# 399 pairs of unread matmuls behind the last sum of squares of an encoder, with weights at sixteen places

## The chip, the cores and the metric

The kernel runs on one core of one Trainium2 chip. The metric is the time of one execution on the device in microseconds. Four compute engines matter: TensorE (PE in the profile; its weight loads are shown as PEld), VectorE (DVE), ScalarE (ACT) and the queue that issues DMAs (SP). GpSimd (POOL) does almost nothing.

## The reference, cut to what matters

The reference is a trunk of two encoder layers on 256 tokens of width 2048, in float32. The end is what the change touches:

```
for i in range(DEPTH):                                   # DEPTH = 2
    h = rmsnorm(x, g_mix[i]);  z = h @ w_in[i]           # then two attentions, gates, w_out
    gu = rmsnorm(x, g_ffn[i]) @ w_gate_up[i]
    x = x + (silu(gate) * up) @ w_down[i]                # D_FF = 5632
    e = p[i] @ w_ple_in[i]
    x = x + sigmoid(rmsnorm(x, g_ple[i]) @ w_ple_gate[i]) * e
return rmsnorm(x, g_final)                               # x * rsqrt(mean(x * x) + eps) * g
```

## The kernel before

The state x is kept transposed in `xT`: 16 chunks of 128 rows (features) by 256 columns (tokens). Each operand of a matmul is a float32 value split into two parts, a rounded high part and the rest: `ua[j]` and `ub[j]` hold one chunk each, 256 columns of high part and then 256 of low part.

A product of weights and activations is written by `product`. It takes the weights in pieces of at most eight blocks of 128x128. For each piece, `piece` issues a DMA into `w` (tag `w32`, four buffers), ACT copies it rounded into `whi` (three buffers, L176), and DVE writes the rest to `wlo` (three buffers). `emit` then issues two matmuls per block, the pair that this document speaks of:

```
PE.matmul(acc, hi[:, s], u, start=start, stop=False)                 # L206: 512 columns
PE.matmul(acc[:, T:], lo[:, s], u[:, :T], start=False, stop=stop)    # L207: 256 columns
```

The first operand after the bank is the stationary one, the weights; `s` starts at a multiple of 128 elements. The bank `acc` is one of four in the pool `ps_mm`. `joined` adds its two halves with the help of ACT. The very last product of the kernel is written with three matmuls of 256 columns per block instead (L202 to L204), so that no joining is needed behind it. In `values` the roles are exchanged: there the activations (`ua`) are the stationary operand and the weights stream (L387 to L389).

The order of the instructions on each engine is made by a scheduler that simulates the program while it is built; a buffer that is asked for again waits until its last reader is done. Each engine works through its own list in order.

The kernel ends like this. In the second layer's last loop each chunk of `xT` gets its last addition, ACT squares it (L258, for the last chunk L255), DVE adds the squares, and ACT scales the chunk by the final gain (L678). `norm` sums over the partitions with four matmuls of one column (L266) and takes the inverse root on DVE; `spread` brings it to all partitions with a matmul by `ones` (L275). Then DVE multiplies `xT` by it in six parts, and each part is sent out by a DMA (L699).

Of the kernel before, what the change touches and what calls it, by code (L numbers as in the profile page):

```python
# [13 lines left out]
F32R = mybir.dt.float32r  # L14
I32 = mybir.dt.int32
AF = mybir.ActivationFunctionType
# [3 lines left out]
P = 128  # L20
T = 256
DM = 2048
NC = DM // P
# [13 lines left out]
PT = 8  # L37
# [13 lines left out]
def encoder(ctx, tc, x, p, positions, cols, lams, wq, wk, wv, wcq, wckv, wkr, wga, wgb,  # L51
            w_q_up, w_kn, w_v, w_bd, w_bm, w_out, w_gate, w_up, w_down, w_pin, w_pg, rope_c, out):
    nc = tc.nc
    V, A, PE = nc.vector, nc.scalar, nc.tensor
# [3 lines left out]
    wts = pool("wts")  # L58
    tmp = pool("tmp")
    stat = pool("stat")  # L60
    ps_mm = pool("ps_mm", 4, space=PSUM)
# [6 lines left out]
    def bank(ps=ps_at, tag="at", name="at", shape=(P, 2 * T)):  # L68
        return ps.tile(list(shape), F32, tag=tag, name=name)

    def tt(o, a, b, op):
        return V.tensor_tensor(out=o, in0=a, in1=b, op=op)  # L72
# [4 lines left out]
    def ts(o, a, s1, s2, op0, op1=ALU.bypass):  # L77
        return V.tensor_scalar(out=o, in0=a, scalar1=s1, scalar2=s2, op0=op0, op1=op1)  # L78


    ua = [const.tile([P, 2 * T], F32R, name=f"ua{j}") for j in range(NC)]
# [12 lines left out]
    xT = const.tile([P, NC, T], F32, name="xT")  # L94
# [18 lines left out]
    aside = [fa(j) for j in range(5)]  # L113
    posi = aside[0][:, 0, :].bitcast(I32)
    posf = aside[0][:, 1, :]

    def tables():
        V.tensor_copy(posf, posi)
        got = []
        for i, name in enumerate("pm"):  # L120
            ang, k, r, a = (aside[j + i][:, m, :] for j in (1, 3) for m in range(2))
            ts(ang, posf, rc[:, 2 * i : 2 * i + 1], None, ALU.mult)
            ts(k, ang, 1.0 / TWO_PI, ROUND, ALU.mult, ALU.add)
            ts(k, k, ROUND, None, ALU.subtract)
            stt(r, k, -C1, ang, ALU.mult, ALU.add)
            stt(r, k, -C2, r, ALU.mult, ALU.add)
            stt(r, k, -C3, r, ALU.mult, ALU.add)
            ts(r, r, PI_IN, -PI_IN, ALU.min, ALU.max)
            stt(a, r, -1.0, r, ALU.mult, ALU.min)
            ts(a, a, math.pi / 2, None, ALU.add)  # L130
            cs = const.tile([P, T], F32, name="cos_" + name)
            sn = const.tile([P, T], F32, name="sin_" + name)
            A.activation(cs, a, AF.Sin)
            A.activation(sn, r, AF.Sin)
            ts(sn, sn, rc[:, 2 * i + 1 : 2 * i + 2], None, ALU.mult)
            got += [cs, sn]
        return got
# [71 lines left out]
    def product(src, us, whole=False):  # L209


        acc = bank(ps_mm, "mm", "mm")
        n = len(us)
        for a in range(0, n, PT):
            m = min(PT, n - a)
            hi, lo = piece(src[:, a * P : (a + m) * P], m)
            emit(acc, hi, lo, 0, us[a : a + m], a == 0, a + m == n, whole)
        return acc[:, :T] if whole else acc
# [10 lines left out]
    def joined(acc, o=None):  # L229
        t = scratch("join", 3)  # L230
        A.activation(t, acc[:, T:], AF.Copy)  # L231
        o = scratch("a", 4) if o is None else o
        tt(o, acc[:, :T], t, ALU.add)
        return o
# [7 lines left out]
    def rsqrt(src, n, eps, width):  # L242

        v, y, a = (stat.tile([P, 2 * DH], F32, tag="r" + s, name="r" + s, bufs=2)[:, :width] for s in "vya")
        ts(v, src, 1.0 / n, eps, ALU.mult, ALU.add)
        ts(y.bitcast(I32), v.bitcast(I32), -0.5, 1597463007.0, ALU.mult, ALU.add)
        for _ in range(3):
            stt(a, y, -0.5, y, ALU.mult, ALU.mult)
            tt(a, a, v, ALU.mult)
            stt(y, a, 1.5, y, ALU.add, ALU.mult)  # L250
        return y

    def square_into(acc, src, first):
        if first:
            A.activation(acc, src, AF.Square)  # L255
        else:
            sq = scratch("sq", 2)
            A.activation(sq, src, AF.Square)  # L258
            tt(acc, acc, sq, ALU.add)

    def norm(sums, n):

        s = bank()
        for j, a in enumerate(sums):
            for b in range(2):
                PE.matmul(s[:, b : b + 1], a[:, b * P : (b + 1) * P], ones[:, 0:1], start=j + b == 0, stop=j + b == len(sums))  # L266
        return rsqrt(s[:, 0:2], n, EPS, 2)

    def spread(col, copied=True):

        dg = stat.tile([P, 2, P], F32, tag="dg", name="dg", bufs=1)
        for b in range(2):
            ts(dg[:, b, :], ident, col[:, b : b + 1], None, ALU.mult)
        s = bank()
        PE.matmul(s[:, :T], ones, dg, start=True, stop=True)  # L275
        if not copied:
            return s[:, :T]
        row = stat.tile([P, T], F32, tag="row", name="row", bufs=2)
        A.activation(row, s[:, :T], AF.Copy)  # L279
        return row  # L280

    def normed(sums, one, two):

        got = [joined(one())]
        col = norm(sums, DM)
        got.append(joined(two()))
        return spread(col), col, got
# [4 lines left out]
    def stream(us, gain):  # L292

        acc = squares()

        def add(c):
            split(us[c], xT[:, c, :], g(gain, c))
            square_into(acc, xT[:, c, :], c == 0)

        return acc, add  # L300
# [110 lines left out]
    for L in range(DEPTH):  # L411

        steps = values(wv[L], ua, None if L else load)
        for vd in steps:
            if L == 0 and vd is not None:
# [3 lines left out]
                with after_splits():  # L419
                    rcol = norm([sq0[0][:, j, :] for j in range(2)], DM)  # L420
                    next(steps)
                    R = spread(rcol)
                    cos_p, sin_p, cos_m, sin_m = tables()
                    lambdas()
                break
            if L:
                next(steps)
                rcol = norm([acc], DM)
                next(steps)
                R = spread(rcol)  # L430
                break
# [5 lines left out]
        for o, t in ((cr, cos_p), (sr, sin_p), (crm, cos_m), (srm, sin_m)):  # L437
            tt(o, t, R, ALU.mult)

# [17 lines left out]
        def latent(us, w, raws):  # L457
            ss = squares()
            for c in range(len(us)):
                tt(raws[c], joined(product(w[L, c], ua)), R, ALU.mult)  # L460
                square_into(ss, raws[c], c == 0)
# [55 lines left out]
        def gate(w, store, n):  # L517
            tt(store(n), joined(product(w[L, n], ua)), R, ALU.mult)

# [115 lines left out]
        acc, add = stream(ub, f"g_ffn{L}")  # L635
# [4 lines left out]

        R, _, pre = normed([acc], lambda: product(w_gate[L, 0], ub), lambda: product(w_up[L, 0], ub))
        pT, es = ua[14:], []
# [4 lines left out]
        for part, (f0, f1) in enumerate(FF_PARTS):  # L647
# [11 lines left out]
            if last:  # L659
                acc, add = stream(ub, f"g_ple{L}")  # L660
# [10 lines left out]
        R, _, pre = normed([acc], lambda: product(w_pg[L, 0], ub), lambda: product(w_pg[L, 1], ub))  # L671
# [8 lines left out]
        else:  # L680
            acc, add = stream(ua, f"g_mix{L + 1}")
# [11 lines left out]
            add(n)  # L693

    R = spread(norm(sums, DM), copied=False)
    for n, m in ((0, 1), (1, 1), (2, 2), (4, 4), (8, 4), (12, 4)):
        o = xT[:, n : n + m, :]
        tt(o, o, R[:, None, :].to_broadcast([P, m, T]), ALU.mult)
        nc.sync.dma_start(out[:, n : n + m, :], o)  # L699
# [84 lines left out]
```

## Time and profile before

| | |
|---|---|
| median of 2 runs | 2934.06 us (2933.75 to 2934.36) |
| the profiled execution | 2934.72 us |
| its span, first to last instruction | 2932.9 us |
| PE busy | 2914.7 us, 99% of the span |
| PEld busy | 2550.8 us, 87% |
| DVE busy | 2063.6 us, 70% |
| ACT busy | 1524.5 us, 52% |
| HBM read | 527.43 MB |

The profile is of one execution. A record has a start and a duration; records of matmuls overlap, because a matmul begins before the results of the one ahead have all left the array. So the pace of a stream of matmuls is read from their starts. The granted clock is the share of TensorE's full clock that the chip let it have in a stretch. Some records of matmuls are missing.

### The profile page before, as it was taken

The page shows a single profiled execution, that of the slowest core. Times are in us where ns is not written, and L with a number is a line of the kernel's source. Part 1 is how long each engine was busy: PE and PEld are TensorE (multiplying, and loading weights), DVE is VectorE, ACT ScalarE, POOL GpSimd, SP SyncE. Part 2 cuts the span into 40 slices and gives each one's busy share as a digit, 9 for nine tenths or more (in the row PEclk, how much of TensorE's full clock was granted, in tenths as well). Part 3 has the DMA queues.
Part 4 walks back from the last instruction along what each step waited for, and adds up shares of the span by engine and source line. Part 5 has one row for each costly group of instructions (what it writes and reads, how often), then busy time and mean ns, then how long its engine had stood idle before and what let it go on. Part 6 is the DMA issues. An engine that isn't in the chain of part 4 may idle for free.

```text
span 2932.9 us, 43979 instructions
## 1 busy us (share of the span) xinstructions
PE 2914.7 (99%) x16750; PEld 2550.8 (87%) x16750; DVE 2063.6 (70%) x3529; ACT 1524.5 (52%) x2529; POOL 1.6 (0%) x8
## 2 busy tenths in 40 slices
PE   9999999999999999999999999999999999999998
PEld 7888888888888888888888888888888888888887
DVE  7897658776666666666859975687666666666676
ACT  6676545544444444445646755455444444444454
POOL 0000000000000000000000000000000000000000
PEclk9999999999999999999999999999999999999999
DMA  6444455555565565555554444555555655655654
GB/s 229 166 161 148 158 188 191 187 186 187 183 193 188 178 191 195 187 187 186 187 186 165 150 153 164 189 190 186 187 187 182 192 188 181 194 188 188 188 185 140
DMA packets 156019, 532.40 MB, mean 182 GB/s; under 512 B 16928, under 2 KB 23840, under 8 KB 155808
## 3 DMA queue, kind: packets, MB, share of 16 engines
q1 hardware_dynamic: 155376, 529.01, 54.5%
q8 instruction: 131, 2.15, 0.3%
q14 instruction: 80, 0.66, 0.1%
q10 hardware_dynamic: 432, 0.59, 0.1%
HBM read 527.43 MB, written 2.10 MB: 181 GB/s over the span
## 4 chain that ended last, share of the span: by engine, by line
PE 99%; DVE 1%; DMA 0%; ACT 0%; SPq 0%; issue 0%; DVEq 0%
PE mm L206 61%; PE mm L207 31%; PE S L336 1%; PE mmv L389 1%; PE mmv L387 1%; PE mmv L388 1%; PE at L354 0%; PE at L558 0%; PE at L615 0%; DMA w<-in_wv 0%; PE at L275 0%; DVE xT L72 0%; PE at L266 0%; DVE wlo L72 0%; DVE a L72 0%; PE at L573 0%
## 5 line engine op out<-in xcount | busy, mean ns | idle before, releaser
L72 DVE TENSOR_TENSOR wlo<-w,whi 128x1024 fp32r<-128x1024 f32 (+2 forms) x1029 | 1229.3, 1195 | 761.6 <-ACT whi L176 749.3
L176 ACT ACTIVATE whi<-w 128x1024 fp32r<-128x1024 f32 (+2 forms) x1029 | 1066.0, 1036 | 1336.4 <-issue 783.8
L206 PE MATMUL mm<-ub,whi 128*128 128x512 f32 x3952 | 1391.3, 394 | 0.0
L206 PE MATMUL mm<-ua,whi 128*128 128x512 f32 x3744 | 1320.3, 394 | 0.0
L207 PE MATMUL mm<-ub,wlo 128*128 128x256 f32 x3952 | 1117.7, 283 | 0.0
L207 PE MATMUL mm<-ua,wlo 128*128 128x256 f32 x3744 | 1059.5, 283 | 0.0
L206 PEld LDWEIGHTS mm<-ub,whi 128*128 128x128 f32 x3952 | 742.0, 188 | 170.3
L206 PEld LDWEIGHTS mm<-ua,whi 128*128 128x128 f32 x3744 | 702.5, 188 | 158.1
L207 PEld LDWEIGHTS mm<-ub,wlo 128*128 128x128 f32 x3952 | 743.2, 188 | 0.8
L207 PEld LDWEIGHTS mm<-ua,wlo 128*128 128x128 f32 x3744 | 704.1, 188 | 2.0
L72 DVE TENSOR_TENSOR a<-mm,join 128x256 f32<-128x256 f32 x421 | 175.2, 417 | 0.3 <-ACT join L231 0.2
L231 ACT ACTIVATE join<-mm 128x256 f32<-128x256 f32 x453 | 166.8, 369 | 5.4 <-PE mm L207 5.1
L72 DVE TENSOR_TENSOR xT<-xT,mm 128x256 f32<-128x256 f32 x256 | 106.9, 420 | 49.6 <-PE mm L207 45.8
L72 DVE TENSOR_TENSOR a<-a,row 128x256 f32<-128x256 f32 x207 | 87.3, 424 | 6.6 <-ACT row L279 0.8
L387 PE MATMUL mmv<-whi,ua 128*128 128x512 f32 x128 | 51.5, 403 | 2.6 <-ACT whi L176 2.6
L72 DVE TENSOR_TENSOR a<-a 128x256 f32<-128x256 f32 x120 | 50.9, 425 | 4.0
L388 PE MATMUL mmv<-whi,ua 128*128 128x512 f32 x128 | 50.9, 399 | 0.0
L72 DVE TENSOR_TENSOR ua<-a,ua 128x256 fp32r<-128x256 f32 x120 | 50.1, 417 | 1.0 <-ACT ua L239 1.0
L239 ACT ACTIVATE ua<-a 128x256 fp32r<-128x256 f32 x120 | 48.4, 403 | 2.6 <-DVE a L72 2.6
L389 PE MATMUL mmv<-wlo,ua 128*128 128x512 f32 x128 | 47.7, 405 | 0.1
L345 ACT ACTIVATE E<-S,nm 128x256 f32<-128x256 f32 x96 | 44.2, 470 | 5.1 <-DVE nm L78 5.0
L72 DVE TENSOR_TENSOR ssq<-ssq,sq 128x256 f32<-128x256 f32 x97 | 40.5, 418 | 0.5 <-ACT sq L258 0.5
(153 smaller groups left out, 1160.3 us busy)
## 6 DMA issues: line engine op xcount, KB each, us to landing
w<-in_w_gate SPq DMA_DIRECT2D x176, 512.0 KB, 4.5
w<-in_w_up SPq DMA_DIRECT2D x176, 512.0 KB, 4.5
w<-in_w_down SPq DMA_DIRECT2D x128, 512.0 KB, 3.5
w<-in_wga SPq DMA_DIRECT2D x64, 512.0 KB, 3.7
w<-in_wgb SPq DMA_DIRECT2D x64, 512.0 KB, 4.4
w<-in_w_out SPq DMA_DIRECT2D x64, 512.0 KB, 4.5
w<-in_w_pg SPq DMA_DIRECT2D x64, 512.0 KB, 3.7
w<-in_w_down SPq DMA_DIRECT2D x64, 384.0 KB, 3.5
```

The lines of the kernel that those rows point to most:

```text
L72: return V.tensor_tensor(out=o, in0=a, in1=b, op=op)
L176: last_split[:] = A.activation(hi[:, :m], w[:, :m], AF.Copy), tt(lo[:, :m], w[:, :m], hi[:, :m].bitcast(F32), ALU.subtract)
L206: PE.matmul(acc, hi[:, s], u, start=start, stop=False)
L207: PE.matmul(acc[:, T:], lo[:, s], u[:, :T], start=False, stop=stop)
L231: A.activation(t, acc[:, T:], AF.Copy)
L239: return A.activation(hi, src, AF.Copy), tt(lo, src, hi.bitcast(F32), ALU.subtract)
L336: PE.matmul(S[:, b, :], q[:, b * P : (b + 1) * P], k, start=j == 0, stop=j == len(pairs) - 1)
L345: last_exp[0] = A.activation(E[:, b, :], S[:, b, :], AF.Exp, bias=nm[:, b : b + 1], scale=scale, accum_out=sm[:, b : b + 1])
L387: PE.matmul(banks[b], xh, hi[:, s], start=a + j == 0, stop=False)
L388: PE.matmul(banks[b], xl, hi[:, s], start=False, stop=False)
L389: last_mm[:] = [PE.matmul(banks[b], xh, lo[:, s], start=False, stop=a + j == n - 1)]
```

## The change

A function `others` is called between the last spreading and the six output products. It takes two buffers of the tag of `whi` and two of the tag of `wlo` and lets ACT copy the first four chunks of `xT` (1024 columns) into each of the four. Then it issues 19 groups of 21 pairs of matmuls, 798 in all, in a fixed order. Each group has a bank of its own from the pool of four; nothing reads it.

A pair is as in `emit`: 512 columns of `ua` with a block of weights from the one tile, and 256 columns with a block from the other, into the second half of the bank. The difference is where the block starts. In the kernel it starts at multiples of 128 elements; here it starts `h` elements further for the first matmul of a pair and `l` further for the second. In eleven groups both are the same (96, 104, 112, 120, 0, 8, 16, 32, 48, 64, 80), in five they differ; that makes sixteen places. Three groups more repeat 96, and do 96 and 0 with the second matmul writing the first half of the bank instead of the second. The output of the kernel is not affected.

```
+    def others():
+        N = 21
+        src = xT[:, :4, :].rearrange("p c t -> p (c t)")
+        his = [wts.tile([P, PT * P], F32R, tag="whi", name="side", bufs=3) for _ in range(2)]
+        los = [wts.tile([P, PT * P], F32R, tag="wlo", name="side", bufs=3) for _ in range(2)]
+        for t in his + los:
+            A.activation(t, src, AF.Copy)
+
+        def blocks(name, h, l, low=T):
+            acc = bank(ps_mm, "mm", name)
+            for j in range(N):
+                k = j % 14
+                o = k % 7 * P
+                tc.keep_in_program_order(PE.matmul(acc, his[k // 7][:, o + h : o + h + P], ua[j % NC], start=j == 0, stop=False))
+                tc.keep_in_program_order(PE.matmul(acc[:, low : low + T], los[k // 7][:, o + l : o + l + P], ua[j % NC][:, :T], start=False, stop=j == N - 1))
+
+        for h in (96, 104, 112, 120, 0, 8, 16, 32, 48, 64, 80):
+            blocks(f"both{h}_", h, h)
+        for h, l in ((96, 0), (0, 96), (96, 32), (96, 112), (112, 96)):
+            blocks(f"h{h}l{l}_", h, l)
+        blocks("again96_", 96, 96)
+        blocks("front96_", 96, 96, 0)
+        blocks("front0_", 0, 0, 0)
...
     R = spread(norm(sums, DM), copied=False)
+    others()
     for n, m in ((0, 1), (1, 1), (2, 2), (4, 4), (8, 4), (12, 4)):
         o = xT[:, n : n + m, :]
         tt(o, o, R[:, None, :].to_broadcast([P, m, T]), ALU.mult)
```

## The prediction

> **What bounds the kernel now.** I read the page first, for the engine that is full and for the clock that it is granted.
>
> ```profile
> span 2932.9 us, 43979 instructions
> PE 2914.7 (99%) x16750; PEld 2550.8 (87%) x16750; DVE 2063.6 (70%) x3529; ACT 1524.5 (52%) x2529; POOL 1.6 (0%) x8
> PEclk9999999999999999999999999999999999999999
> ...
> PE 99%; DVE 1%; DMA 0%; ACT 0%; SPq 0%; issue 0%; DVEq 0%
> ...
> L206 PE MATMUL mm<-ub,whi 128*128 128x512 f32 x3952 | 1391.3, 394 | 0.0
> ...
> L207 PE MATMUL mm<-ub,wlo 128*128 128x256 f32 x3952 | 1117.7, 283 | 0.0
> ```
>
> TensorE is busy for 2914.7 of 2932.9 us, and the chain that ended last is 99% PE. The kernel is one stream of pairs: a matmul of 512 columns (L206) and one of 256 (L207), each with its own block of weights. The change adds 399 pairs of just this shape, so the number wanted is the price of one more pair. It is not the mean of a record: 394 and 283 ns add up to 677, but the records overlap. The price is the distance from start to start, which the timeline of PE shows. Its columns are start, duration (both us), engine, line, operation.
>
> ```profile
> 2900.18 0.40 PE L206 MATMUL mm<-ub,whi 128*128 128x512 f32 x1
> ...
> 2908.61 0.40 PE L206 MATMUL mm<-ub,whi 128*128 128x512 f32 x1
> 2908.61 0.19 PEld L207 LDWEIGHTS mm<-ub,wlo 128*128 128x128 f32 x1
> ...
> 2908.84 0.28 PE L207 MATMUL mm<-ub,wlo 128*128 128x256 f32 x1
> 2908.85 0.19 PEld L206 LDWEIGHTS mm<-ub,whi 128*128 128x128 f32 x1
> 2908.97 0.40 PE L206 MATMUL mm<-ub,whi 128*128 128x512 f32 x1
> ...
> 2910.72 0.40 PE L206 MATMUL mm<-ub,whi 128*128 128x512 f32 x1
> ```
>
> Between 2900.18 and 2910.72 lie 30 pairs without a gap: 10.54 / 30 = **0.3513 us a pair**. Inside one, the short matmul starts 0.23 after the long one and the next long one 0.12 to 0.13 after that. The load of the next weights begins as its predecessor's matmul begins, so loads lie under matmuls.
>
> The second thing is the end of the kernel, where the new work goes.
>
> ```profile
> 2908.69 1.06 ACT L176 ACTIVATE whi<-w 128x1024 fp32r<-128x1024 f32 x1 [0.62 <-PE mm L206]
> ...
> 2911.30 0.28 PE L207 MATMUL mm<-ub,wlo 128*128 128x256 f32 x1
> ...
> 2911.62 0.38 ACT L231 ACTIVATE join<-mm 128x256 f32<-128x256 f32 x1 [1.57 <-PE mm L207]
> ...
> 2914.15 0.28 PE L204 MATMUL mm<-ub,wlo 128*128 128x256 f32 x1
> ...
> 2917.77 0.42 ACT L690 ACTIVATE sig<-a 128x256 f32<-128x256 f32 x1 [2.49 <-DVE a L72]
> ...
> 2919.60 0.61 PE L266 MATMUL at<-ones,ssq 128*128 128x1 f32 x4 [1.99 <-ACT ssq L255]
> ...
> 2922.94 1.22 PE L275 MATMUL at<-dg,ones 128*128 128x256 f32 x2 [2.73 <-DVE dg L78]
> 2924.20 4.74 DVE L72 TENSOR_TENSOR xT<-xT,at 128x256 f32<-128x256 f32 x6 [1.31 <-PE at L275]
> 2924.65 4.65 SPq L699 DMA_DIRECT2D out_y<-xT  x6
> ```
>
> After the last product PE does only the sum over partitions (L266) and the spreading of its root (L275). From 2924.16 (2922.94 + 1.22) PE has nothing left, and 8.7 us go to DVE's six products and six DMAs.
>
> **The change part by part.** In the built order every DMA and every instruction ahead of the end stands as before, but for what is named here.
>
> *The four copies on ACT.* They stand among the last steps, ahead of the last sigmoid. Each is 128x1024 from f32 to fp32r, the form of L176, so 1.06 us; they need buffers of whi and wlo that the fourteenth product frees when its last matmul ends (2911.30 + 0.28 = 2911.58) and the first half of the fifteenth frees at about 2914.4. From 2911.58 ACT then has 4 x 1.06 = 4.2 us of copies, and six steps of 0.38 to 0.51, about 2.7: it is free for the last sigmoid at about 2918.4 if it never waits. Now the sigmoid starts at 2917.77. So the end moves by about 0.5 us; 0 if the steps overlap, some 2 if a copy that waits for 2914.4 holds up the sigmoid queued behind it. DVE swaps one product with one sum of squares; that lets the last sigmoid's input come no later. I take 0.5.
>
> *The 798 matmuls.* In PE's order they all stand behind L275. Their inputs (ua, the copies) have long been there by then, and the banks are written but never read, so nothing on PE waits. DVE's products and the output's DMAs run beside them and are over at about 2933, so the 8.7 us of tail are cover, and PE becomes the end.
>
> First PE needs a start. The second pass of L275 is out of the way at about 2924.0, with the 0.5 at 2924.5. Then the clock: the stretches view gives the granted clock of any stretch (it stands ahead of the DMA share).
>
> ```profile
> 12.05:15.46 3.41, 3.36 (x8) 2.72 (x9) 3.41 (x6) 3.34 (x6) 0.00 (x0) 0.50 1.03 409
> 15.46:18.90 3.44, 3.44 (x16) 2.78 (x16) 3.18 (x6) 2.41 (x4) 0.00 (x0) 1.00 0.98 359
> ...
> 2920.21:2932.90 12.69, 1.22 (x3) 0.50 (x2) 7.00 (x19) 0.00 (x0) 0.00 (x0) 0.50 0.43 165
> ```
>
> From 2920.2 on, the clock is at half, since PE has hardly worked from 2917.3 on: the new matmuls start slowly. How slowly, and for how long, the start of the kernel shows, where the clock fell too:
>
> ```profile
> 13.12 0.63 PE L387 MATMUL mmv<-whi,ua 128*128 128x512 f32 x1
> ...
> 14.82 0.63 PE L388 MATMUL mmv<-whi,ua 128*128 128x512 f32 x1
> ```
>
> Four steps in 1.70 us: 0.425 for 512 columns, so about 0.64 for a pair at half clock. The slow stretch was 3.41 long there. Whether the clock comes back after one such stretch or at the end of the second is a matter of where the work falls in it: 3.4 to 6.8 us, and I take the middle, 5.1. That is 8 pairs at 0.64; at full speed they would have taken 2.8, so the loss is 2.3 us (1.6 to 3.1).
>
> The other 391 pairs at 0.3513 take 137.4 us. After the last start comes 0.28 instead of 0.12: 0.2. **The sum:** 2924.5 + 5.1 + 137.4 + 0.2 = 3067.2. Around the span the profiled execution has 2934.72 - 2932.9 = 1.8, so 3069.0; it stands 0.66 above the median of 2934.06, so **3068**, 4.6% more.
>
> *The places of the weights* are what the trace of before shows only in part. All blocks of L206 and L207 start at a multiple of 128 elements in their tile, as in the groups both0 and front0; in the other 17 groups (357 pairs) at least one of the two weights is shifted by 8 to 120 elements. What rows are there with weights elsewhere? L387 to L389 take theirs from ua, which in the built program's layout is offset, against whi and wlo, by just what a shift of 96 gives.
>
> ```profile
> 16.98 0.39 PE L387 MATMUL mmv<-whi,ua 128*128 128x512 f32 x1
> ...
> 25.34 0.39 PE L387 MATMUL mmv<-whi,ua 128*128 128x512 f32 x1
> ...
> 208.88 0.38 PE L573 MATMUL at<-ident,fa 128*128 128x128 f32 x2
> ```
>
> Of these 36 matmuls of 512 columns lie between the two starts: 8.36 / 36 = 0.232, against the 0.23 that L206 takes. L573 loads from fa, offset as a shift of 104 gives: two matmuls end 0.38 after the first starts, and one lasts 0.27, so they are 0.11 apart. A load that is not aligned as whi is thus still issued at 0.11 or faster. Two of the places cost nothing, then, and for all I take the price of both0. From below: 512 columns at half clock took 0.425, so at full clock the columns alone need 0.2125 and 0.106, 0.319 a pair: 0.032 less, and no less than that, since the columns are there. From above: a load twice as long (0.22) would still fit under a long matmul's 0.23 but not under the short one's 0.12, and would add 0.10 to a pair. The forecast is at the low end of these because that is where the two rows lie.
>
> The Trainium skill ("TensorE: Matmul & The Clock Gate", section "Back-to-back issue gap") gives the distance of two isolated matmuls at full clock as columns / 2.4 GHz + 2.5 ns, that is 216 and 109 ns; an estimate by that page is 325 ns a pair and 3058 for the whole. This case's trace does not agree for aligned weights: 0.351.
>
> **The rivals.**
>
> *Pairs without the stall.* Of a pair, 0.032 us is not columns. If that comes from where the load reads while the matmul reads ua, another place may free it. All 17 groups: 357 x 0.032 = 11.4 us less, 3057; a few groups: some 3 us less. For it: nothing in the rows tells what the 0.032 is. Against: the 36 matmuls with weights in ua keep 0.232, so that place at least isn't free of it. The page's rule above is the extreme of this one.
>
> *Some places load slower.* Under the 256 columns there is 0.12 us, and an aligned load already uses 0.11 of it: hardly any slack, so a load even a fifth longer shows in full. Twice as long in all 17 groups: 357 x 0.10 = 36 us more, 3104; a fifth longer (0.02): 7 us, 3075; half the groups at twice: 3086. Against: L573 and L387. For: only two of the fifteen shifts have a row.
>
> *The unread matmuls don't run*, the rival on the other side. Nobody reads the 19 groups; if they were left out, or ran beside the tail, the time would be 2934 + 0.5 for the copies. The tail covers 8.7 us and 2% is 58.7, together 67 us or 192 pairs: this rival decides once fewer than 192 of the 399 run, or a pair takes under 0.169. Against: all 798 stand in the built order of PE, and 0.169 is half of what the columns alone need.
>
> **How the numbers follow.** About 2% is what a measurement of this kernel can tell from no change: 59 us, less than half of the forecast's 134. Forecast, a pair within some 3% of 0.351 for the mean of the groups, 3064 to 3074: 0.60. Faster pairs, 3056 to 3064: 0.13. Slower loads, 3074 to 3104: 0.22. Not run: 0.01. Anything else (a clock that stays low longer, a larger wait on ACT): 0.04. The range of 8 in 10 reaches to the mild half of both rivals: 3059 (a pair of 0.33 on average) to 3082 (0.385). Slower by over 2%: 0.985; within 2%: 0.01; faster: 0.005.
>
> **What the profile after would show.** PE with 798 more matmuls and a span near 3067; up to about 2917 nothing changed; the last sigmoid 0 to 2 us later; half clock from about 2920 until 3.4 to 6.8 us after the first new matmul; then 0.351 from start to start in both0 and front0. The last point is the one to read: if the 19 groups, about 7.4 us each, differ, the place of the weights has a price, and the sum errs by 21 times the difference in every such group. The forecast is wrong if the differences have one sign and exceed 0.03 a pair, or if PE waits between groups.

## The result, and the profile after

The changed kernel takes 3066.78 us (two runs, 3065.9 and 3067.66) against 2934.06: 1.0453 times as long, 95% interval 1.0432 to 1.0473. The profiled execution had 3065.9 us. The page of the changed kernel, the lines that answer to those shown of before (here L233 and L234 are the pair that was L206 and L207):

```profile
span 3064.1 us, 45579 instructions
PE 3054.9 (100%) x17548; PEld 2676.1 (87%) x17548; DVE 2064.1 (67%) x3529; ACT 1528.3 (50%) x2533; POOL 1.6 (0%) x8
...
PE 99%; DVE 1%; DMA 0%; ACT 0%; SPq 0%; issue 0%; DVEq 0%
...
L233 PE MATMUL mm<-ub,whi 128*128 128x512 f32 x3952 | 1391.3, 394 | 0.0
```

PE has 17548 - 16750 = 798 matmuls more and 140.2 us more of busy time; ACT has four instructions more. The chain is still PE.

The timeline of the end, changed kernel (start, duration, engine, line, operation):

```profile
2909.31 0.27 PE L229 MATMUL mm<-ub,whi 128*128 128x256 f32 x1
2909.39 1.06 ACT L126 ACTIVATE side<-xT 128x1024 fp32r<-128x1024 f32 x1 [1.45 <-PE mm L233]
...
2915.65 0.42 ACT L717 ACTIVATE sig<-a 128x256 f32<-128x256 f32 x1 [0.17 <-DVE a L72]
...
2917.49 1.02 PE L293 MATMUL at<-ones,ssq 128*128 128x1 f32 x4 [0.88 <-ACT ssq L282]
...
2921.24 1.22 PE L302 MATMUL at<-dg,ones 128*128 128x256 f32 x2 [2.74 <-DVE dg L78]
2921.90 0.99 PE L133 MATMUL both__29159<-ua,side 128*128 128x512 f32 x1
2922.50 4.74 DVE L72 TENSOR_TENSOR xT<-xT,at 128x256 f32<-128x256 f32 x6 [1.31 <-PE at L302]
...
2922.90 0.63 PE L133 MATMUL both__29159<-ua,side 128*128 128x512 f32 x1
...
2924.18 0.47 PE L133 MATMUL both__29159<-ua,side 128*128 128x512 f32 x1
...
2924.61 0.40 PE L133 MATMUL both__29159<-ua,side 128*128 128x512 f32 x1
...
2930.51 0.39 PE L133 MATMUL both__29202<-ua,side 128*128 128x512 f32 x1
...
2945.32 0.40 PE L133 MATMUL both__29288<-ua,side 128*128 128x512 f32 x1
...
2952.61 0.40 PE L133 MATMUL both__29331<-ua,side 128*128 128x512 f32 x1
...
2959.98 0.40 PE L133 MATMUL both__29374<-ua,side 128*128 128x512 f32 x1
...
3033.78 0.39 PE L133 MATMUL h112l__29804<-ua,side 128*128 128x512 f32 x1
...
3040.92 0.40 PE L133 MATMUL again__29847<-ua,side 128*128 128x512 f32 x1
...
3055.77 0.39 PE L133 MATMUL front__29933<-ua,side 128*128 128x512 f32 x1
...
3063.01 0.28 PE L134 MATMUL front__29933<-ua,side 128*128 128x256 f32 x1
```

The six output products and their DMAs run beside the new matmuls, as the forecast had it. The names in the rows are cut at the number; in order, 2945.32 starts both120, 2952.61 both0, 2959.98 both8, 3033.78 the group 112/96, 3040.92 again96. From 2930.51 to 3055.77 lie 17 groups, 357 pairs: 125.26 / 357 = 0.3509 us a pair. But the groups differ: both120 has 7.29 / 21 = 0.347, both0 7.37 / 21 = 0.351, the group 112/96 7.14 / 21 = 0.340. The first pairs of a group differ; from about its middle on, the distances from start to start repeat in a fixed order. By their mean there, both104, both112, both16, both32, both48, both80, 96/32, again96 and front96 have 353.3 ns, both0, both64 and front0 351.1, 0/96 352.0, both8 and 96/0 350.0, both96, both120 and 96/112 346.7, and 112/96 340.0. front96 and front0 are like again96 and both0: which half of the bank is written makes no difference. But both96 and again96, the same place twice, are not alike: 346.7 and 353.3.

For the clock, the stretches view of the changed kernel (the granted clock stands ahead of the DMA share):

```profile
12.05:15.46 3.41, 3.41 (x17) 2.75 (x16) 2.74 (x5) 3.02 (x6) 0.00 (x0) 1.00 1.03 411
2917.53:2924.33 6.80, 4.06 (x13) 3.51 (x14) 4.09 (x17) 0.45 (x1) 0.00 (x0) 0.50 0.06 20
2924.35:3064.10 139.75, 138.94 (x793) 121.20 (x791) 2.89 (x3) 0.00 (x0) 0.00 (x0) 1.00 0.04 15
```

### The profile page after: what moved, and what is told of

It reads as the page before. It is cut to its first block, busy times and chain, and to the rows that moved or that the text cites. A ratio compares the mean times of both kernels' runs of the same rounds, so it can differ in the third digit from the quotient of the medians.

```text
span 3064.1 us, 45579 instructions
## 1 busy us (share of the span) xinstructions
PE 3054.9 (100%) x17548; PEld 2676.1 (87%) x17548; DVE 2064.1 (67%) x3529; ACT 1528.3 (50%) x2533; POOL 1.6 (0%) x8
## 4 chain that ended last, share of the span: by engine, by line
PE 99%; DVE 1%; DMA 0%; ACT 0%; SPq 0%; issue 0%; DVEq 0%
PE mm L233 58%; PE mm L234 30%; PE S L363 1%; PE mmv L416 1%; PE mmv L414 1%; PE mmv L415 1%; PE at L381 0%; PE at L585 0%; PE at L642 0%; DMA w<-in_wv 0%; PE at L302 0%; PE both__29159 L133 0%; PE both__29460 L133 0%; PE front__29890 L133 0%; PE again__29847 L133 0%; PE h96l__29718 L133 0%
## 5 line engine op out<-in xcount | busy, mean ns | idle before, releaser
L233 PE MATMUL mm<-ub,whi 128*128 128x512 f32 x3952 | 1391.3, 394 | 0.0
L233 PE MATMUL mm<-ua,whi 128*128 128x512 f32 x3744 | 1320.3, 394 | 0.0
L234 PE MATMUL mm<-ub,wlo 128*128 128x256 f32 x3952 | 1118.9, 283 | 0.0
L234 PE MATMUL mm<-ua,wlo 128*128 128x256 f32 x3744 | 1060.6, 284 | 0.0
L233 PEld LDWEIGHTS mm<-ub,whi 128*128 128x128 f32 x3952 | 742.2, 188 | 169.0
L233 PEld LDWEIGHTS mm<-ua,whi 128*128 128x128 f32 x3744 | 702.8, 188 | 157.0
L234 PEld LDWEIGHTS mm<-ub,wlo 128*128 128x128 f32 x3952 | 744.3, 188 | 0.8
L234 PEld LDWEIGHTS mm<-ua,wlo 128*128 128x128 f32 x3744 | 705.2, 188 | 2.0
L266 ACT ACTIVATE ua<-a 128x256 fp32r<-128x256 f32 x120 | 48.5, 404 | 2.6 <-DVE a L72 2.6
```

The costliest lines, as they stand in the source:

```text
L266: return A.activation(hi, src, AF.Copy), tt(lo, src, hi.bitcast(F32), ALU.subtract)
```

## The experiments

The sum came out; what it rested on without a row was the price of a pair at the places of the weights. So the experiments ask what sets that price, and whether the kernel itself can be had at a better one. Each run with groups behind the last sum is one profiled execution; the changed kernels without groups were timed several times beside the kernel before on the same chip.

### A map of places

```
-        for h in (96, 104, 112, 120, 0, 8, 16, 32, 48, 64, 80):
-            blocks(f"both{h}_", h, h)
...
+        for w in range(2):
+            blocks(f"warm{w}_", 0, 0)
+        for h in range(0, 64, 8):
+            for l in range(0, 64, 8):
+                blocks(f"h{h}l{l}_", h, l)
```

> In place of the 19 groups stand two groups to warm up and then 64 groups of 21 pairs: the first matmul's weights start h elements past a multiple of 128, the second's l, both from 0, 8, ... 56. Theory A (the pace of a pair is set by the places of both weights, modulo 64 elements, together): the seven pairs of places that the changed kernel shared with this map come out as there, (0,0) 0.351 us a pair, (8,8) 0.350, (16,16) 0.353, (32,32) 0.353, (48,48) 0.353, (32,48) 0.347, (48,32) 0.340, (56,56) 0.347, and the rest lies between 0.337 and 0.356 in a pattern. Theory B (a place has a price of its own, and the two add up): the map is a sum of a row's and a column's price, within 0.001; against it speaks already that (48,32)+(32,48) is 0.687 and (32,32)+(48,48) 0.706. Theory C (the differences belong to the time, not to the place: what DMAs or the clock did while the group ran): (48,32) is not below 0.349.

Read in the same way, in ns a pair: (0,0) 351.1, (8,8) 350.0, (16,16) 348.9, (32,32) 346.7, (48,48) 353.3, (32,48) 346.7, (48,32) 350.0, (56,56) 346.7. Five of the eight agree; (32,32), (16,16) and (48,32) do not. The timeline of the map, the first matmul of the group (48,32) and of the next:

```profile
3321.49 0.39 PE L133 MATMUL h48l__31481<-ua,side 128*128 128x512 f32 x1
...
3328.84 0.39 PE L133 MATMUL h48l__31524<-ua,side 128*128 128x512 f32 x1
```

7.35 / 21 = 0.350 here, where the same distance had 0.340 in the group 112/96 above. So theory A is wrong for some places: they have more than one pattern. Theory B is wrong too: the sum over (0,0) and (32,32) is 697.8, over (0,32) and (32,0) 698.7, but (8,8)+(16,16) is 698.9 and (8,16)+(16,8) 702.7. What theory C said of (48,32) came true, but it does not explain why (0,0) came out at 351.1 and (56,56) at 346.7 here and in every later run with that distance from the columns. What shows in the whole map is that some paces are preferred: 24 of the 64 groups have 346.7 ns and 11 have 353.3. At half clock two pairs of the changed kernel took 1.28 us (2922.90 to 2924.18 above), 0.64 for the 768 columns of a pair; by that, the columns alone are estimated at 320 ns a pair at full clock, and 16 columns at 6.67. The expectations below call these 6.67 ns a quantum: 340.0, 346.7 and 353.3 are 51, 52 and 53 of them. It describes the common paces and is not shown to be more: the other groups lie between, at (0,0) the pairs are 354, 354 and 345 long in turn, in the kernel before as well, and at (16,32) every pair takes 350.

### Other starts of the columns

```
+        mv = wts.tile([P, PT * P], F32R, tag="w32", name="moving", bufs=W_BUFS)
+        A.activation(mv, src, AF.Copy)
...
+                tc.keep_in_program_order(PE.matmul(acc, his[k // 7][:, o + h : o + h + P], mv[:, m : m + 2 * T], start=j == 0, stop=False))
```

> The columns that stream come from a tile of their own and start m elements past a multiple of 64, m = 0, 8, 16, 32, 48, 56; ua starts where m = 32 does. For each m eight groups. Theory D (the two reads of PE, weights and columns, meet in the memory, so that only the differences h-m and l-m count, modulo 64): for every m the group (h,l) = (m+16, m) has 0.340 us a pair, (m, m+16) 0.347, (m+32, m+32) 0.351, (m+24, m+24) 0.347, while (48,32) is at 0.340 for m = 32 alone. Theory E (the weights' own place counts, where the columns start does not): (48,32) has 0.340 for every m, (32,48) 0.347, (0,0) 0.351, (56,56) 0.347, and the four others change with m.

The timeline of this run, first matmuls of groups: with the columns at m = 0 the group (32,32) and the next; at m = 32 the group (48,32) twice and the next; at m = 56 the group (24,24) and the next.

```profile
2974.45 0.39 PE L137 MATMUL m0h32l__29462<-moving,side 128*128 128x512 f32 x1
...
2981.82 0.39 PE L137 MATMUL m0h56l__29505<-moving,side 128*128 128x512 f32 x1
...
3113.79 0.40 PE L137 MATMUL m32h48l__30279<-moving,side 128*128 128x512 f32 x1
...
3120.94 0.39 PE L137 MATMUL m32h48l__30322<-moving,side 128*128 128x512 f32 x1
...
3128.08 0.40 PE L137 MATMUL m32h32l__30365<-moving,side 128*128 128x512 f32 x1
...
3266.84 0.39 PE L137 MATMUL m56h24l__31182<-moving,side 128*128 128x512 f32 x1
...
3274.21 0.39 PE L137 MATMUL m56h56l__31225<-moving,side 128*128 128x512 f32 x1
```

7.37 / 21 = 0.351 at m = 0 and at m = 56 for two quite different places of the weights that are both 32 elements away from the columns. For all six m the groups with the distance 32 had 351.1 or 351.2 ns, those with 24 346.7, and those with 0 for the first and 16 for the second matmul 346.7. The place (48,32) had 340.0 at m = 32 alone (7.15 / 21), and 346.7 to 353.3 at the others; 340.0 came once more, unforeseen, for (32,48) at m = 48. Theory E is out. Theory D holds for these three distances and not for the fourth: (m+16, m) had 340.0 at m = 0, 32 and 56 and 350.0 at 8, 16 and 48. Other groups of this run show the same: with both weights at a distance of 0, 346.7 at m = 0 and 353.3 at m = 56; at 8, 353.3 at m = 56 and 346.7 at m = 48; at 48, 348.9 at m = 16 and 353.3 at m = 8. Such distances have more than one pattern, which also fits the map, where the very same place came out in two ways; what chooses between them these runs don't show.

### Weights with a step, columns in halves

```
+            return t[:, at : at + P] if step == 1 else t[:, at : at + (P - 1) * step + 1 : step]
...
+                return mv[:, m : m + 2 * n : 2]
+            return mv[:, : 2 * n].rearrange("p (l r) -> p l r", r=64)[:, :, m : m + 32]
```

> The first two runs left this theory: while a load reads weights, the matmul in front reads columns of the same memory; the pair lasts a whole number of quanta of 6.67 ns (16 columns at full clock), 51, 52 or 53 of them, against 48 for the columns alone, and only the distance of the two addresses counts, modulo 64 elements. Theory F (the memory has banks, and the two readers move through them at different speeds, so they must meet, each meeting one quantum): here the weights of a block are taken with a step of 1, 2, 3 or 4 elements, and the columns from all of a tile, from half of each 64 elements, or with a step of 2. With weights at a step of 2 both move at the same speed; after at most one meeting they stay apart: 0.320 to 0.333 us a pair at most distances, against 0.351 (place 0) and 0.347 (place 56) at a step of 1. Columns with a step of 2 bring the difference back: over 0.34. Theory G (a fixed cost of changing the weights, 3 to 5 quanta, whose exact size depends on an alignment): step 2 gives 0.340 to 0.354 like step 1. Theory H (strided weights are slower to load): step 2, 3, 4 give more than 0.36, rising.

The timeline, first matmuls: a group with weights at a step of 2 and the next, a group with a step of 4 and the next.

```profile
2954.57 0.40 PE L146 MATMUL two__29333<-moving,side 128*128 128x512 f32 x1
...
2962.03 0.40 PE L146 MATMUL two__29376<-moving,side 128*128 128x512 f32 x1
...
3100.27 0.51 PE L146 MATMUL four__30150<-moving,side 128*128 128x512 f32 x1
...
3110.20 0.52 PE L146 MATMUL four__30193<-moving,side 128*128 128x512 f32 x1
```

Theory F fell: at a step of 2 the 16 groups have 346.7 to 360.0 ns (the one shown 7.46 / 21 = 0.355), none near 0.333. Theory G is left, with four groups of step 2 a little above its bound at 355.5 or 355.6 and one at 360.0. Theory H fails for a step of 2 and holds for steps of 3 and 4: 410 to 411 and 470 to 473 ns. With a step of 3, PEld is busy without a break (10.00 of 10.00 us, 5.32 of 6.00 with a step of 2), so the loads seem to set the pace there, one behind the other, 0.205 or 0.235 each on average. That is the price that the second rival was afraid of; a mere shift doesn't cause it. The Trainium skill ("SBUF — State Buffer", section "Specifications (TRN2)") says that full bandwidth needs two hits on a line of 16 bytes; a step of 2 still has two hits, 3 and 4 have not, and for the weights the trace agrees. For the columns it does not: at a step of 2 they have two hits as well, and took twice their time (680 to 687 ns a pair). Columns from one half of each 64 elements had 353.3 to 357.8.

### Fewer weight columns, and a finer map

```
+        def blocks(name, h, l, N=13, cols=P):
...
+        for cols in (128, 96, 64, 32):
+            for h, l in ((0, 0), (56, 56), (48, 32), (32, 32)):
+                blocks(f"cols{cols}h{h}l{l}_", h, l, 21, cols)
+        for h in range(0, 64, 4):
+            for l in range(0, 64, 4):
+                blocks(f"h{h}l{l}_", h, l)
```

> First 16 groups at four places, where the block of weights has 128, 96, 64 or 32 columns; then 256 groups of 13 pairs with both places in steps of 4 elements. Theory I (what a pair takes beyond its 320 ns of columns comes from the loads, line by line, as they read beside the columns): at (0,0) 31 ns at 128 weight columns, 23 at 96, 16 at 64, 8 at 32. Theory G (a fixed cost of each change of weights, rounded up to a quantum by the alignment of addresses): 20 to 33 ns at all four. In the map: groups whose places are multiples of 8 repeat the first map where the pace is one of (0,0) 351.1, (24,24) 346.7, (56,56) 346.7, (32,48) 346.7 ns; (48,32) may come out as 340.0, 350.0 or 353.3, as it did before. If some places keep to 340.0 ns or less, they are to be seen as a block of neighbours in the map; if 340.0 is only one of several states of a place, it stands scattered.

At (0,0) the pair had 351.1, 346.7, 346.7 and 340.0 ns with 128, 96, 64 and 32 weight columns; at the other three places 32 columns gave 344.4 to 348.8. The group with 32 columns at (0,0), and the start of the next:

```profile
3019.56 0.39 PE L133 MATMUL cols32h0l__29729<-ua,side 128*32 128x512 f32 x1
...
3026.70 0.40 PE L133 MATMUL cols32h56l__29772<-ua,side 128*32 128x512 f32 x1
```

7.14 / 21 = 0.340. A quarter of the load leaves at least 20 of the 31 ns, and at (32,32) 64 weight columns had 340.0 but 32 more than that: not theory I. Theory G foretold these numbers, but a fixed cost of each change of weights is not shown. No run streams matmuls that keep their weights, and two paces speak against a fixed cost: at half clock a pair takes the same 0.427 and 0.213 us for its 512 and 256 columns, with nothing left over for each matmul, and with the columns at a step of 2 a pair takes 40 to 47 ns more than 640, twice the time of its columns, where theory G has 20 to 33. In the finer map no group is below 340.0; three of 256 have it, far apart, (16,36), (48,4) and (48,36), while (48,32) had 350.0 this time. So 340.0 stands scattered.

### The kernel with its weights moved

The same edit with four pairs of shifts, without the 798 matmuls, and once with the wider buffers alone (shown: 48 and 32):

```
-        hi = wts.tile([P, PT * P], F32R, tag="whi", name="whi", bufs=3)
-        lo = wts.tile([P, PT * P], F32R, tag="wlo", name="wlo", bufs=3)
+        hi = wts.tile([P, PT * P + 64], F32R, tag="whi", name="whi", bufs=3)[:, 48 : 48 + PT * P]
+        lo = wts.tile([P, PT * P + 64], F32R, tag="wlo", name="wlo", bufs=3)[:, 32 : 32 + PT * P]
```

> The kernel before, without the 798 matmuls, but with the buffers of whi and wlo 64 elements wider and all weights shifted by 48 elements in whi and by 32 in wlo. If the place sets the pace in the kernel as in the group h112l96 (340.0 ns a pair), 7696 pairs are 11.1 ns shorter each: 85 us, 2849 us, ratio 0.971. Rival: in the kernel ACT, DVE and DMAs use the memory too and the pace is theirs, or PE then waits for weights: 2925 to 2935, ratio 0.997 to 1.0.

> The same with both shifted by 32, the place that the changed kernel had in the groups both32, both96 and again96 (353.3 ns a pair). If the place sets the pace: 7696 pairs are 2.2 ns longer each, 17 us, 2951 us, ratio 1.006. Rival (a wider buffer, or any shift, does what e3 shows): the same time as e3. Rival (the place does nothing in the kernel): 2934.

> The kernel before with all weights shifted by 56 elements in whi and wlo. In every group with this distance (24 elements from the columns, in nine groups so far, at six starts of the columns) the pair had 346.7 ns, where the place of the kernel before had 351.1. If the place works in the kernel as in the groups: 7696 pairs of 4.4 ns, 34 us: 2899 us, ratio 0.988. If only the width of the buffers or any shift works, as in the runs with 48/32 and 32/32: 2927, ratio 0.998.

> The kernel before with the buffers of whi and wlo 64 elements wider, as in the three runs with shifted weights, and no shift. If the shift is what made those faster: pairs at 0.351 and 2934 us, ratio 0.999 to 1.001. If the wider buffers (the other addresses of all that lies behind them) did it: 2903 to 2927, ratio 0.990 to 0.998.

> The same with whi shifted by 48 and wlo by 4, one of the three scattered places of the fine map with 340.0 ns. If a place holds its state: 7696 pairs 11.1 ns shorter, 2849 us, ratio 0.971. If 340.0 is one of several states of a place and a stream leaves it at the next disturbance (theory of scattered states): a mean of 347 to 352 in the kernel, 2903 to 2941, ratio 0.99 to 1.002, not faster than the shift by 56 with 2903.

| shift of whi / wlo | time, us | ratio to before (95%) | mean pair, ns |
|---|---|---|---|
| 0 / 0, wider only | 2934.08 | 0.9998 (0.9988 to 1.0008) | 351.0 |
| 48 / 32 | 2926.11 | 0.9976 (0.9967 to 0.9985) | 350.2 |
| 32 / 32 | 2927.81 | 0.9982 (0.9972 to 0.9991) | 350.5 |
| 48 / 4 | 2912.06 | 0.9925 (0.9910 to 0.9940) | 348.1 |
| 56 / 56 | 2903.32 | 0.9896 (0.9880 to 0.9913) | 346.8 |

The last column is the mean over the pairs of the profiled run that follow each other without a gap; the kernel before has 351.0. The gain of 56/56, 4.3 ns times 7696 pairs = 33 us, is the 31 that were measured, and 2.9 ns x 7696 = 22 for 48/4 are its 23. The wider buffers alone do nothing. The first expectation, 2849 for 48/32, was wrong by 77 us, and so was 2951 for 32/32, on the other side of before: both places have at least two patterns each, and a stream of products changes between them. The 2926.11 lies where the rival of that expectation had it, that the kernel's pace is set by others; the run with 56/56, which gained nearly what the groups promised, speaks against this rival. At 48/4 the change of pattern shows in one execution; the timeline of two stretches of 60 pairs:

```profile
2150.26 0.39 PE L206 MATMUL mm<-ub,whi 128*128 128x512 f32 x1
...
2170.66 0.39 PE L206 MATMUL mm<-ub,whi 128*128 128x512 f32 x1
...
2400.13 0.39 PE L206 MATMUL mm<-ub,whi 128*128 128x512 f32 x1
...
2421.13 0.39 PE L206 MATMUL mm<-ub,whi 128*128 128x512 f32 x1
```

20.40 / 60 = 0.340, and later 21.00 / 60 = 0.350 with the same places. The pace does not wander. In each of the runs with 48/32, 32/32 and 48/4 there are 24 streams of 20 pairs or more in which long and short matmuls take strict turns; all of them keep one pace from end to end, and it changes only where the turn is broken, as where two long matmuls follow each other between these two stretches. At 56/56, and at the place of before, every long unbroken stretch keeps one pace.

### The kernel with its columns moved

The sharpest test of the distance: leave the weights alone and move `ua` and `ub` by 8 elements, then move both by 24.

```
+    ahead = const.tile([P, 8], F32, name="ahead")
     ua = [const.tile([P, 2 * T], F32R, name=f"ua{j}") for j in range(NC)]
     ub = [const.tile([P, 2 * T], F32R, name=f"ub{j}") for j in range(NC)]
+    behind = const.tile([P, 64 - 8], F32, name="behind")
+    nc.gpsimd.memset(ahead, 0.0)
+    nc.gpsimd.memset(behind, 0.0)
```

> The kernel before with ua and ub moved 8 elements up in memory and nothing else; the weights stay where they are. The distance of weights and columns, 32 elements before, becomes 24, as in the run with the weights shifted by 56 (64 - 8 = 56). If only the distance counts: 346.7 ns a pair and 2903 us, ratio 0.990. If the weights' own place counts: 351.1 ns and 2934.

> Weights shifted by 24 elements in whi and wlo, ua and ub moved up by 24 too: both lie elsewhere, the distance is that of before. If only the distance counts: 351.1 ns a pair and 2934 us, ratio 0.999 to 1.001. If a place of its own counts: any other time; 24 was a place with 346.7 ns in the first map, which would give 2900.

With the columns moved by 8: 2902.72 us, ratio 0.9892 (0.9876 to 0.9909). With both moved by 24: 2934.08, ratio 0.9999 (0.9989 to 1.0008). At these two distances only the distance counts: 24 gives 2902.72 here and 2903.32 with the weights moved, 32 gives 2934.86 in the kernel before on that chip and 2934.08 with both moved. The timeline of the first of them, 60 pairs apart (L210 is the long matmul there):

```profile
2400.04 0.39 PE L210 MATMUL mm<-ub,whi 128*128 128x512 f32 x1
...
2420.84 0.39 PE L210 MATMUL mm<-ub,whi 128*128 128x512 f32 x1
```

20.80 / 60 = 0.3467. This version is faster than both kernels, by 1.1% than the one before, with 256 bytes of padding in each partition.

## Why the prediction was right, point by point

**The price of a pair.** 0.3513 was forecast for all, 0.3509 came out as the mean. For both0 and front0 the forecast was right as argued, 0.351. For the others it was right in the mean only, and that is luck: nine groups were 2 ns dearer and a few 1 to 11 ns cheaper. The argument from L387 to L389 could not have shown this. It looked at the place of the weights alone; but their columns come from `whi`, so by the prediction's own layout (96, that is 32 modulo 64) weights and columns are 32 elements apart there, as in the kernel before. And the shift of 96 that this row stood for came out at 346.7 and 353.3.

**The clock: the step that failed.** The forecast counted 3.4 to 6.8 us at half clock *from the first new matmul*, and took 5.1. It lasted 2.4, from 2921.90 to 2924.34. What repeats is the length of the whole stretch from the fall of the clock, 6.83 us, twice 3.41: it began at 2917.5, long before the new matmuls. In the four other runs with groups at the end the slow stretch is as long, 6.8 us at 0.50, while from their first new matmul it lasted 2.2 to 3.4. Counted so, the forecast's own rows (the fall at 2920.20, the first new matmul at 2924.5) give 2.5. The work that ended it stood in its second half, where PE was busy from 2921.24 on. The Trainium skill ("TensorE: Matmul & The Clock Gate", section "Part 1: The HAM clock gate") has windows of 3413 ns that run freely and a full clock after a busy one; the trace agrees, 3.41 twice. Four pairs began in 2.71 us instead of 1.40: the loss was 1.3, not 2.3.

**The start.** 2921.90, where 2924.5 was forecast. Most of that, 2.1 us, is not of the change: the last product began at 2909.31, in the profiled run of before it was this row:

```profile
2911.43 0.27 PE L202 MATMUL mm<-ub,whi 128*128 128x256 f32 x1
```

At the beginning the kernel before had lost time at half clock in 12.05:15.46, and the changed one had 1.00 there; 3.41 us at half clock cost at most 1.7, the rest I can't place. In the map run, which has the same copies and a slow stretch at its beginning, the last product began at 2911.45.

The four copies on ACT cost nothing, where 0.5 was forecast: the last sigmoid starts 6.34 us behind the first matmul of the last product in both kernels (2917.77 - 2911.43 and 2915.65 - 2909.31). From that matmul to the spreading went 11.51 us before and 11.93 after, but these 0.4 come behind the sigmoid: the four matmuls that sum over the partitions took 1.02 (L293, at 2917.49) instead of 0.61 (L266), because the clock fell at 2917.5, just as they began; before it fell at 2920.20, as they ended. Two runs show that it is the clock and not the copies. The kernel with wider buffers alone has no copies and half clock from 2918.63 on; the run with steps in the weights has five copies and full clock until 2919.99 (the two rows in this order):

```profile
2918.71 1.01 PE L266 MATMUL at<-ones,ssq 128*128 128x1 f32 x4 [1.99 <-ACT ssq L255]
...
2919.47 0.60 PE L319 MATMUL at<-ones,ssq 128*128 128x1 f32 x4 [0.88 <-ACT ssq L308]
```

So the 0.5 for the copies was nearly met, by luck, by another cost that the forecast did not have. The first new matmul began 0.66 behind the start of the spreading, not 1.06.

**The end.** The last matmul ends at 3063.29, the span 0.8 later, which the forecast had left out. Together: -2.6 for the start, -1.0 for the clock, -0.2 for the pairs, +0.8 for the end is -3.0: the span was forecast at 3067.2 and was 3064.1. That the median was met within 1.2 us is partly luck: the 2.1 of the start is a difference between executions that the forecast couldn't know, and the profiled execution lies 0.9 below the median here, it lay 0.7 above it before.

**The rivals.** Pairs without the stall: no group of shifted weights went below 0.340, and the 0.325 of the estimate for isolated matmuls was seen in none of the runs. Slower loads: shown for steps of 3 and 4, not for shifts. Not run: all 798 are in the trace.

What stays open is why a pair costs 340 to 353 ns and not the 320 estimated for its columns, why the distance of two addresses modulo 64 elements decides between them, and why a place with two patterns takes the one or the other when the turn of long and short matmuls starts anew. A meeting of two readers in banks of the memory was argued and fell with the step of 2.

## What to carry to other kernels

Price added work by the distance from start to start in a stream of the same form, not by the durations of records, and then look at the ends: the clock, the tail that covers it, what stands behind. Where matmuls change their weights each time, the distance in memory between weights and columns is a knob: here moving the columns by 8 elements gave 1.1%. Choose a distance that showed one pace in every repetition; the fastest group of a sweep may be one of several patterns that the kernel doesn't keep.

## What the runs showed of the hardware

The pace of a pair of fp32r matmuls (512 and 256 columns, new weights for each) was 340 to 356 ns at full clock, most often 346.7 or 353.3, and 640 at half clock. At two distances of the operands' starts, modulo 64 elements (256 bytes), it was the same wherever they lay: 351.1 at 32 for both weights and 346.7 at 24, in every group and kernel that had it with whole blocks of weights. Other distances had two paces or more. With a quarter of the weight columns the pair costs 340.0 to 348.8. With weights at a step of 2 it takes 346.7 to 360.0 ns, at 3 and 4 0.41 and 0.47 us. Four matmuls of one column with their loads took 0.61 us at full clock and 1.02 at half. In the five runs with work behind the last sum the half clock lasted 6.83 us from its fall.
